# RWKV time mixing: keys and values with features on the partitions, low ranks from the unmixed input, and an earlier token reorder

## The chip, the cores and the metric

One NeuronCore of a Trainium2 chip runs the whole program. The metric is device microseconds (us) of one execution; a kernel's time is the median of its runs. TensorE is called PE below (PEld is its weight load), VectorE is DVE, ScalarE is ACT, GpSimd is POOL, and SP is the SyncE queue that issues every DMA of this kernel.

## What is computed

Two transformer blocks over one sequence of T = 512 tokens with 1024 features. The first block has neighbourhood attention on an 8 x 64 grid of tokens, a gated convolution and an MLP. The second has two layers with a feed-forward net (SwiGLU) ahead of and behind a mixer; the mixer of its first layer is the RWKV-7 time mixing, which the change is about:

```python
x_prev = jnp.pad(x, ((0, 0), (1, 0), (0, 0)))[:, :-1]
xx = x_prev - x
xr, xw, xk, xv, xa, xg = [x + xx * mu[i] for i in range(6)]
r = xr @ w_rkv[0]; k = xk @ w_rkv[1]; v = xv @ w_rkv[2]
w = -jax.nn.softplus(-(w0 + jnp.tanh(xw @ w1) @ w2)) - 0.5
decay = jnp.exp(-jnp.exp(w))
a = jax.nn.sigmoid(a0 + (xa @ a1) @ a2)
g = jax.nn.sigmoid(xg @ g1) @ g2
kk = heads(k * k_k); kk = kk / jnp.maximum(norm(kk), 1e-12)   # per head of 64
k = k * (1.0 + (a - 1.0) * k_a)
# scan over t, per head, S is 64 x 64:
#   S = S * w_t + (S @ -kk_t) b_t^T + v_t k_t^T ;  y_t = S @ r_t
# then group norm, bonus, gate g, and @ w_o
```

w1 and a1 have 64 columns, g1 has 128; the matrices of r, k, v and w_o are 1024 x 1024.

## The kernel before

Activations lie transposed, features on the 128 partitions and tokens along the free dimension, in eight tiles of 128 x 512 (`DC` = 8). The large products are exact to fp32 through a split: `wload` brings 128 x 1024 weights by DMA (`wr`), ACT rounds them to a high part (`wh`), DVE or POOL subtracts for the low part (`wl`), and `mm3` issues three matmuls (high by high, high by low, low by high). The first block runs with its tokens in column order of the grid; the time mixing needs them in sequence.

The program is written as one main stream of products and as side tasks (Python generators). A planner (`_Emit`) places the side tasks between the main products; its result is one fixed order of instructions on each engine, and each engine's queue is then strictly in order. All DMAs go through the SP queue, in order too: a store that waits for its data holds up the loads behind it.

The time mixing (`rwkv`) works in two halves of 256 tokens, hf = 0 and 1. `norm_task` makes, for each feature chunk c, a tile `ud` with u (the normalised input) and its shift difference d. `mix_task` makes the mixtures u + d * mu on DVE: for K, R and V each chunk is also split in high and low (ACT, then POOL or DVE), for the low ranks W, A and G it is not. Then the main stream runs through `ORDER`:

```python
ORDER = [(0, K_), (0, W_), (0, A_), (0, R_), (0, V_), (0, G_), (1, K_), (1, W_), (1, A_), (1, R_), (1, V_), (1, G_)]
```

K and V go through `token_major`: tokens on the partitions, the mixture as the stationary operand, 512 columns of weights moving, four PSUM banks at once; `keys_task` scales, norms and transposes the keys, `values_task` transposes the values. R goes through `receptance`, the other way round: 128 x 128 weights stationary, 256 tokens moving. The low ranks go through `lora1`, fp32 matmuls of 256 tokens by 64 or 128 weight columns whose weights `load_raw` has fetched one or two steps ahead. All results go to DRAM (`spill`) and are fetched again by blocks of 128 tokens j = 0 to 3 and halves of the heads q = 0, 1.

Behind this runs a chain of side tasks for each block j: `prep(q, j)` (DVE and ACT, small matmuls on PE), for which K, the decay, A and R of that half must be there (`flags`), room for 12 tiles must be free, and fewer than two are under way; when both q are done, `inverse(j)`, which inverts 32 x 32 triangles in 31 steps of two dependent POOL instructions, after a trip through DRAM (`fsc` out, `iat` in; `xsc` out and in behind it) and three rounds of 32 x 32 matmuls; `scan_task(q)`, two steps of 64 tokens for each j, each a string of small matmuls and DVE work; and `gn_task`. When j = 0 and 1 are through, `w_o(0)` multiplies the first half by the output matrix, and the following feed-forward net (`ffn_halves`) can start on it; the second half's chain then runs beside that net.

The token reorder stands in the first feed-forward net of the second block, `ffn(0, 0, perm=True)`: DVE's products of the hidden values read and write through strided views (`rows_first`, `natural`), and after the first group of hidden values the eight tiles of the residual `h` are copied into sequence order on ACT, with a second set of row statistics (`Stat`).

Of the kernel before, what the change touches and what calls it, by code (L numbers as in the profile page):

```python
# [12 lines left out]
F32 = mybir.dt.float32  # L13
# [7 lines left out]
P = 128  # L21
# [16 lines left out]
def _vec_layout():  # L38
    col = 0
    for name, n in [  # L40
        ("norm1_g", 8), ("norm2_g", 8), ("norm_g", 96), ("conv_w", 12), ("qk_g", 2), ("mu", 48),
        ("a0", 8), ("k_a", 8), ("r_k", 8), ("gn_g", 8), ("gn_b", 8), ("kv_norm_g", 8),
# [14 lines left out]
R_KK, R_BV, R_SINK = 0, 1024, 1280  # L57
# [238 lines left out]
def tile_net(ctx: ExitStack, tc: tile.TileContext, a: dict, out: bass.AP, dbg=None, stop=None):  # L296
# [438 lines left out]

    for n in range(DC):
# [136 lines left out]
    def rows_first(ap):  # L873

        return ap.rearrange("p (c r) -> p r c", r=8)

    def natural(ap):
        return ap.rearrange("p (r c) -> p r c", c=64)

# [103 lines left out]
    def ffn(layer, i, en, on_h=None, perm=False, on_last=None):  # L983
# [10 lines left out]
        for lo_, hi_ in GROUPS:  # L994
            hid, waits = {}, []

            def hidden(j, pg, pu):
# [7 lines left out]
                def fn():  # L1005
                    s_ = A()
                    if perm:
                        tt(vt, natural(s_), rows_first(pg), rows_first(st.rb), MUL)
                        act.activation(out=s_, in_=s_, func=AF.Silu)
                        tt(vt, natural(s_), rows_first(pu), natural(s_), MUL)  # L1010
                    else:
                        tt(vt, s_, pg, st.rb, MUL)
                        act.activation(out=s_, in_=s_, func=AF.Silu)
                        tt(vt, s_, pu, s_, MUL)
# [24 lines left out]
            if lo_ == 0 and perm:  # L1039
                hp_ = []  # L1040
                st = Stat()
                for c in range(DC):
                    t_ = A()
                    copy(natural(t_), rows_first(h[c]))
                    hp_.append(t_)
                    st.add(t_)
                h = hp_
                st_pre = st
                for hf in range(2):
                    em.spawn(st.task(hf, bcast=False))  # L1050
                st = en.st
# [3 lines left out]
            if lo_ == GROUPS[1][0]:  # L1055
                if perm:
                    em.until(st_pre.all)
                    pre = st_pre.y
                else:
                    pre = st.y  # L1060
                so = Stat(pre=pre, post=0.5)
# [54 lines left out]
    def rwkv(on_h):  # L1116
# [23 lines left out]
        def mix_chunk(i, c, hf):  # L1140

            uc, dc, m = ud[hf, c][:, 0:256], ud[hf, c][:, 256:512], V("mu", 8 * i + c)
            if i in LORA:
                if c % 2 == 0:
                    half_tile[0] = A()
# [1019 lines left out]
```

## Time and profile before

| | us |
|---|---|
| median of 3 runs | 2996.33 |
| runs | 2992.95 to 2996.84 |
| the profiled execution | 2992.11 |
| span of its trace | 2990.3 |
| PE busy in the span | 2832.4 (95%) |
| DVE busy | 1623.5 (54%) |
| ACT busy | 1250.4 (42%) |
| POOL busy | 688.6 (23%) |

The profile is of one execution; 1.8 us of its time lie outside the span. PE is busy nearly throughout, so a stage in which it is not stands out: the time mixing, from about 1043 to 1560 us of the span. A busy PE may still be slow, since the clock that it is granted has two levels; tables by stage therefore list the granted clock (1.00 is 2.4 GHz, 0.50 is 1.2 GHz, in between is a mean).

### The profile page before, as it was taken

Reading aid. Unit: us, or ns where it says so; the run is one execution under the profiler, and the core shown is the slowest. Engines: PE = TensorE matmul, PEld = TensorE weight load, DVE = VectorE, ACT = ScalarE, POOL = GpSimd, SP = SyncE. Lnnn points to the kernel's source line nnn. Section 1 sums busy time; section 2 is a strip of 40 time slices with the busy share of each in tenths; the row PEclk is TensorE's granted clock in tenths of the full one; section 3 lists DMA queues with packets and bytes.
Section 4 is the critical chain, followed back from the end, with each engine's and each line's share of the span. In section 5 each row is a group of like instructions: output and inputs, shape, how many; then the busy total and the mean of one; then the engine's idle time right before and its main releaser. Section 6 shows DMA issues by size and latency. Waiting matters only on the chain. (4 is left out here: it accounts for less than half of the span.)

```text
span 2990.3 us, 45732 instructions
## 1 busy us (share of the span) xinstructions
PE 2832.4 (95%) x17744; PEld 2448.3 (82%) x17744; DVE 1623.5 (54%) x2920; ACT 1250.4 (42%) x2157; POOL 688.6 (23%) x809
## 2 busy tenths in 40 slices
PE   9999999999999988688789999998999998999998
PEld 7788988889788877557669999998888887888887
DVE  6544443335334485775866664457334475852336
ACT  4523333333433345455445544344333347743333
POOL 0011211111211143554254110011111126420111
PEclk9999999999999988889779999999999999999999
DMA  5232333332334355555455655343333333323334
GB/s 186 89 99 92 113 105 93 99 99 85 93 99 125 117 178 171 179 177 163 145 169 156 198 174 178 121 156 86 112 99 123 116 115 86 104 84 102 110 109 154
DMA packets 179408, 378.31 MB, mean 127 GB/s; under 512 B 57204, under 2 KB 81908, under 8 KB 179192
## 3 DMA queue, kind: packets, MB, share of 16 engines
q1 hardware_dynamic: 179192, 375.40, 40.5%
q8 instruction: 140, 2.29, 0.3%
q14 instruction: 76, 0.62, 0.1%
HBM read 342.04 MB, written 29.36 MB: 124 GB/s over the span
## 5 line engine op out<-in xcount | busy, mean ns | idle before, releaser
L377 PE MATMUL m<-a,wh 128*128 128x256 f32 (+1 forms) x8512 | 2068.2, 335 | 7.2 <-DVE a L288 4.8
L377 PEld LDWEIGHTS m<-a,wh 128*128 128x128 f32 x8512 | 1463.7, 192 | 171.8 <-issue 8.4
L377 PE MATMUL m<-a,wl 128*128 128x256 f32 (+1 forms) x4256 | 1415.3, 333 | 3.6 <-DVE wl L288 3.3
L288 ACT ACTIVATE wh<-wr 128x1024 fp32r<-128x1024 f32 (+2 forms) x585 | 606.5, 1038 | 1190.6 <-PE m L377 814.6
L288 DVE TENSOR_TENSOR wl<-wr,wh 128x1024 fp32r<-128x1024 f32 (+2 forms) x547 | 672.6, 1231 | 467.7 <-ACT wh L288 464.6
L377 PEld LDWEIGHTS m<-a,wl 128*128 128x128 f32 x4256 | 816.2, 192 | 79.6 <-DVE wl L288 5.0
L288 POOL TENSOR_TENSOR a<-a,a 128x256 f32<-128x256 f32 (+5 forms) x319 | 361.9, 1141 | 1645.6 <-ACT a L288 1321.6
L288 DVE TENSOR_TENSOR a<-m,a 128x512 f32<-128x512 f32 (+1 forms) x324 | 208.3, 644 | 636.6 <-PE m L377 619.0
L288 ACT ACTIVATE a<-a 128x512 f32<-128x512 f32 (+6 forms) x531 | 253.3, 495 | 120.7 <-DVE a L288 101.1
L377 PE MATMUL m<-wh,a 128*128 128x512 f32 x800 | 269.6, 412 | 22.4 <-POOL a L288 9.5
L377 PEld LDWEIGHTS m<-wh,a 128*128 128x128 f32 x800 | 156.5, 197 | 63.2 <-POOL a L288 11.8
L288 DVE TENSOR_TENSOR a<-a,a 128x256 f32<-128x256 f32 (+3 forms) x305 | 165.5, 569 | 25.1 <-ACT a L288 18.2
L377 PE MATMUL m<-wl,a 128*128 128x512 f32 x400 | 162.6, 406 | 0.2 <-DVE wl L288 0.2
L288 DVE SCALAR_TENSOR_TENSOR a<-a,vec,a 128x256 fp32r<-128x256 f32 (+4 forms) x246 | 147.7, 640 | 8.6 <-ACT a L288 8.3
L288 POOL TENSOR_TENSOR a<-h,a 128x256 fp32r<-128x256 f32 x80 | 68.1, 855 | 293.2 <-ACT a L288 277.8
L288 POOL TENSOR_TENSOR wl<-wr,wh 128x1024 fp32r<-128x1024 f32 x38 | 92.8, 2444 | 129.1 <-ACT wh L288 97.8
L377 PE MATMUL t<-a,a 64*128 64x128 f32 (+4 forms) x528 | 91.8, 361 | 31.8 <-DVE a L288 21.8
L377 PEld LDWEIGHTS t<-a,a 64*128 64x128 f32 (+3 forms) x528 | 59.3, 202 | 57.5 <-issue 24.5
L288 ACT ACTIVATE a<-t 128x512 f32<-128x512 f32 (+3 forms) x122 | 58.5, 490 | 95.3 <-PE t L377 73.3
L377 PEld LDWEIGHTS m<-wl,a 128*128 128x128 f32 x400 | 78.8, 197 | 16.9 <-issue 0.7
L288 ACT ACTIVATE a<-a,vec 128x256 fp32r<-128x256 f32 (+2 forms) x108 | 60.3, 566 | 41.3 <-DVE a L288 39.2
L290 ACT ACTIVATE a<-t 128x256 f32<-128x256 f32 (+3 forms) x100 | 45.5, 473 | 65.4 <-PE t L377 47.3
(108 smaller groups left out, 1527.7 us busy)
## 6 DMA issues: line engine op xcount, KB each, us to landing
wr<-in_ffn_w_in_dram SPq DMA_DIRECT2D x204, 512.0 KB, 3.6
wr<-in_ffn_w_out_dram SPq DMA_DIRECT2D x80, 448.0 KB, 3.3
wr<-in_ffn_w_out_dram SPq DMA_DIRECT2D x48, 512.0 KB, 3.5
wr<-in_w_out_t_dram SPq DMA_DIRECT2D x34, 512.0 KB, 3.3
wr<-in_w_mlp_in_dram SPq DMA_DIRECT2D x32, 512.0 KB, 3.5
wr<-in_w_mlp_out_dram SPq DMA_DIRECT2D x32, 512.0 KB, 3.7
wr<-in_w_gate_dram SPq DMA_DIRECT2D x16, 512.0 KB, 3.6
wr<-in_w_k_dram SPq DMA_DIRECT2D x16, 512.0 KB, 4.4
```

The lines of the kernel that those rows point to most:

```text
L288: return fn(*args, **kw)
L290: return fn(*args, **kw)
L377: nc.tensor.matmul(out_, lhsT=lhsT, rhs=rhs, start=start, stop=stop)
```

## The change

Four edits. (1) K and V go through a new function `features`, the form that R had: eight output chunks n, for each 24 matmuls with 128 x 128 weights stationary and 256 tokens moving, one PSUM bank. `keys` squares the keys on ACT, sums them by head with 128 x 2 matmuls on PE, spreads the inverse norms over features by four transposes for each pair of chunks, and multiplies on DVE out of PSUM; `values` (not shown) copies, stores and transposes back for the token-major copy `vd`. The copies in DRAM (`kt`, `kkt`, `vt`) are now by half and chunk, stored as 128 x 256 tiles and fetched in rows of 128 tokens. (2) The low ranks use u and d themselves: x @ w1 with x = u + d * mu is u @ w1 + d @ (mu * w1). POOL scales the weights by mu (`lora1`), W and A share one product with 64 + 64 columns (`wa1`), and the weights are loaded inside `lora1`. (3) `ORDER` is shorter, `AHEAD` is 12 in place of 8 and `EARLY` 8 in place of 10 (of ten steps, not twelve). (4) The reorder moves to the gated sum of the first block: POOL's addition of the two branches reads `rows_first` and writes `natural`; the residual is read from a copy of x in sequence order (`x_nat`); `perm` is gone.

```diff
-        tt(gp, sg[0], sg[0], sg[1], ADD)
-        mg.append(split(sg[0], eng=gp))
+        t_ = A()
+        tt(gp, natural(t_), rows_first(sg[0]), rows_first(sg[1]), ADD)
+        mg.append(split(t_, eng=gp))
     h = []
     for c in range(DC):
         t_ = A()
-        dma(out=t_, in_=a["x"][:, c * T : (c + 1) * T])
+        dma(out=t_, in_=a["x_nat"][:, c * T : (c + 1) * T])
         h.append(t_)
...
-                    if perm:
-                        tt(vt, natural(s_), rows_first(pg), rows_first(st.rb), MUL)
-                        act.activation(out=s_, in_=s_, func=AF.Silu)
-                        tt(vt, natural(s_), rows_first(pu), natural(s_), MUL)
...
-            if lo_ == 0 and perm:
-                hp_ = []
-                st = Stat()
-                for c in range(DC):
-                    t_ = A()
-                    copy(natural(t_), rows_first(h[c]))
-                    hp_.append(t_)
-                    st.add(t_)
-                h = hp_
-                st_pre = st
-                for hf in range(2):
-                    em.spawn(st.task(hf, bcast=False))
-                st = en.st
...
-        LORA = {W_: ("w1", 64), A_: ("a1", 64), G_: ("g1", 128)}
-        ORDER = [(0, K_), (0, W_), (0, A_), (0, R_), (0, V_), (0, G_), (1, K_), (1, W_), (1, A_), (1, R_), (1, V_), (1, G_)]
-        LAST_A = [x for x in ORDER if x[0] == 0][-1]
-        mixed = {x: [] for x in ORDER}
+        WA_, L_ = W_, (W_, G_)
+        ORDER = [(hf, i) for hf in range(2) for i in (K_, WA_, R_, V_, G_)]
+        MIXED = [x for x in ORDER if x[1] not in L_]
+        mixed = {x: [] for x in MIXED}
...
-        AHEAD = 8
-        EARLY = 10
+        AHEAD = 12
+        EARLY = 8
...
-        def token_major(w, i, hf):
-            pss = {(wh, jj): PS() for wh in range(2) for jj in range(2)}
-            for k0 in range(0, DC, 2):
-                ws = [wload(w[wh][:, k0 * 512 : (k0 + 2) * 512], 1024, eng=alt()) for wh in range(2)]
-                for k in range(k0, k0 + 2):
+        def features(w, i, hf, fin):
+            for n in range(DC):
+                ps = PS()
+                hi, lo = wload(w[n], 1024, eng=alt())
+                for k in range(DC):
                     xh, xl = take(hf, i, k)
-                    sl = slice((k - k0) * 512, (k - k0 + 1) * 512)
-                    for (wh, jj), ps in pss.items():
-                        hi, lo = ws[wh]
-                        tb = slice(jj * 128, (jj + 1) * 128)
-                        em.need(ps, xh[:, tb], xl[:, tb], hi[:, sl], lo[:, sl])
-                        mm3(ps, xh[:, tb], xl[:, tb], hi[:, sl], lo[:, sl], k == 0, k == DC - 1)
-                    used[0] += 1
-                    free(xh)
+                    sl = slice(k * 128, (k + 1) * 128)
+                    em.need(ps, hi[:, sl], lo[:, sl], xh, xl)
+                    mm3(ps[:, HW], hi[:, sl], lo[:, sl], xh, xl, k == 0, k == DC - 1)
+                    if n == DC - 1:
+                        used[0] += 1
+                        free(xh)
+                fin(n, ps)
             mixed[hf, i] = None
-            return pss
...
-        def lora1(w, m, hf, i):
+        def lora1(hf, name, idx):
+            ws = load_raw(a[name], 1024)
+            ms = []
+            for i, w_ in enumerate(ws):
+                m_ = A()
+                w4, m4 = (t_.rearrange("p (k i m) -> p k i m", k=4, i=len(idx)) for t_ in (w_, m_))
+                for x, id_ in enumerate(idx):
+                    c = _VEC["mu"] + 8 * id_ + 4 * i
+                    mu = vec[:, c : c + 4].unsqueeze(2).broadcast_to([P, 4, 128 // len(idx)])
+                    tt(gp, m4[:, :, x, :], w4[:, :, x, :], mu, MUL)
+                ms.append(m_)
             ps = PS()
             for k in range(DC):
-                x_ = take(hf, i, k)[0]
-                w_ = w[k * m // 512][:, k * m % 512 : k * m % 512 + m]
-                em.need(ps[:m, HW], w_, x_)
-                mm(ps[:m, HW], w_, x_, k == 0, k == DC - 1)
-                if k % 2:
-                    used[0] += 1
-                    free(x_)
-            mixed[hf, i] = None
+                em.until(lambda: (hf, k) in ud)
+                for i, t_ in enumerate((ws, ms)):
+                    w_, x_ = t_[k // 4][:, (k % 4) * 128 : (k % 4 + 1) * 128], ud[hf, k][:, HALF[i]]
+                    em.need(ps[:, HW], w_, x_)
+                    mm(ps[:, HW], w_, x_, k == 0 and i == 0, k == DC - 1 and i == 1)
+            free(*ws, *ms)
             return ps
...
+        def keys(hf):
+            st_ = kst[hf] = {"ss": None, "n": 0}
+            def square(n, sq):
+                yield (sq,)
+                if st_["ss"] is None:
+                    st_["ss"] = PS()
+                for jj in range(2):
+                    c = 16 * jj + 2 * n
+                    mm(st_["ss"][:, c : c + 2], sq[:, jj * 128 : (jj + 1) * 128], bones[:, 0:128:64])
+                st_["n"] += 1
+                if st_["n"] == DC:
+                    em.spawn(norm(st_["ss"]))
+            def norm(ps):
+                s1, s2 = S(), S()
+                v, f, tmp = s1[:, 0:32], s2[:, 0:32], s2[:, 32:64]
+                vt.tensor_scalar(out=v, in0=ps[:, 0:32], scalar1=1e-24, scalar2=None, op0=MAX)
+                rsqrt_(f, v, tmp)
+                for n in range(0, DC, 2):
+                    if n % 4 == 0:
+                        fb = [A(), A()]
+                        for jj in range(2):
+                            c = 16 * jj + 2 * n
+                            copy(fb[jj].rearrange("p (h d) -> p h d", d=64), f[:, c : c + 8].unsqueeze(2).broadcast_to([P, 8, 64]))
+                    yield tuple(fb)
+                    pf = PS()
+                    for i in range(2):
+                        for jj in range(2):
+                            x0 = ((n + i) % 4) * 128
+                            transpose(pf[:, i * 256 + jj * 128 : i * 256 + (jj + 1) * 128], fb[jj][:, x0 : x0 + 128])
+                    if n % 4 == 2:
+                        free(*fb)
+                    k_ = kt.pop((hf, n // 2))
+                    for i in range(2):
+                        kk = H()
+                        vt.scalar_tensor_tensor(out=kk, in0=k_[:, HALF[i]], scalar=V("k_k", n + i), in1=pf[:, HALF[i]], op0=MUL, op1=MUL)
+                        spill(kkd[hf][n + i], kk)
+                    free(k_)
+                    if n % 4 == 2:
+                        flags["k", hf, n // 4] = True
+            def fin(n, ps):
+                if n % 2 == 0:
+                    kt[hf, n // 2] = A()
+                t_, sq = kt[hf, n // 2][:, HALF[n % 2]], H()
+                copy(t_, ps[:, HW])
+                act.activation(out=sq, in_=ps[:, HW], func=AF.Square, scale=V("k_k", n))
+                spill(kd_[hf][n], t_)
+                em.spawn(square(n, sq))
+            return fin
...
-        tasks = {W_: decay_task, A_: a_task, G_: g_task}
-        raw = {}
         for n, (hf, i) in enumerate(ORDER):
-            for nxt in ORDER[n : n + 2]:
-                if nxt[1] in LORA and nxt not in raw:
-                    w, m = LORA[nxt[1]]
-                    raw[nxt] = load_raw(a[w], 8 * m)
             if not hv and n >= EARLY and min(done["z"]) >= 1:
                 w_o(0)
-            if i in LORA:
-                em.spawn(tasks[i](hf, lora1(raw[hf, i], LORA[i][1], hf, i)))
-                free(*raw[hf, i])
+            if i == WA_:
+                ps = lora1(hf, "wa1", (W_, A_))
+                em.spawn(decay_task(hf, ps))
+                em.spawn(a_task(hf, ps))
+            elif i == G_:
+                em.spawn(g_task(hf, lora1(hf, "g1", (G_,))))
+                free(*(ud[hf, c] for c in range(DC)))
             elif i == K_:
-                em.spawn(keys_task(hf, token_major(a["w_k"], K_, hf)))
+                features(a["w_k"], K_, hf, keys(hf))
             elif i == V_:
-                em.spawn(values_task(hf, token_major(a["w_v"], V_, hf)))
+                features(a["w_v"], V_, hf, values(hf))
             else:
-                receptance(hf)
+                features(a["w_r"], R_, hf, receptance(hf))
...
-        ffn(0, 0, en, en_r.add, perm=True, on_last=lambda: next(mixing))
+        ffn(0, 0, en, en_r.add, on_last=lambda: next(mixing))
```

What the edits do to the order of the queues shows at three places. On SP, the place is the end of the first half's keys. Before, the weights of the first low rank (`in_w`) were issued ahead of the last key weights and of all key stores:

```order
L288 DMA wr_8932<-in_w_k_dram 128x1024
L288 DMA wr_8976<-in_w_k_dram 128x1024
L288 DMA a_8741<-in_w_dram 128x512
L288 DMA xsc_8727<-a_8731 128x512 x2
L288 DMA xsc_8728<-a_8731 128x512 x2
L288 DMA xsc_8729<-a_8731 128x512 x2
L288 DMA xsc_8730<-a_8731 128x512 x2
L288 DMA wr_8982<-in_w_k_dram 128x1024
```

Now, on SP at the same place of the program (`kt` is the store of the keys, `in_wa` the joint weights of W and A):

```order
L288 DMA kt_5533<-a_8964 128x256
L288 DMA wr_9437<-in_w_r_dram 128x1024
L288 DMA kt_5533<-a_9074 128x256
L288 DMA wr_9471<-in_w_r_dram 128x1024
L288 DMA kt_5533<-a_9074 128x256
L288 DMA a_9136<-in_wa_dram 128x512
L288 DMA a_9137<-in_wa_dram 128x512
L288 DMA wr_9509<-in_w_r_dram 128x1024
```

The joint weights have moved behind the store of the last key chunk.

On POOL, the place is the end of the first `inverse` (tiles `iat` and its X). Before, the second one followed at once:

```order
L288 TENSOR_TENSOR h_10635<-a_9968,iat_9967 128x16
L288 TENSOR_TENSOR a_9968<-a_9968,h_10635 128x16
L288 MEMSET a_10588 128x512
L288 MEMSET a_10588 64x16 x2
L288 TENSOR_TENSOR h_10721<-a_10588,iat_10587 128x31
L288 TENSOR_TENSOR a_10588<-a_10588,h_10721 128x31
```

Now other work follows the first inverse on POOL (`a<-a,vec` scales low-rank weights, `h<-h,s` is the scan's, `wl` are weights of R and V, 22 rows in all up to the second inverse):

```order
L288 TENSOR_TENSOR h_10680<-a_10079,iat_10078 128x16
L288 TENSOR_TENSOR a_10079<-a_10079,h_10680 128x16
L288 TENSOR_TENSOR wl_11530<-wr_11528,wh_11529 128x1024
L288 TENSOR_TENSOR a_10798<-h_10796,a_10798 128x256
L288 TENSOR_TENSOR a_10814<-h_10812,a_10814 128x256
L288 TENSOR_TENSOR a_10854<-h_10852,a_10854 128x256
L288 TENSOR_TENSOR a_10859<-h_10857,a_10859 128x256
L288 TENSOR_TENSOR wl_11746<-wr_11744,wh_11745 128x1024
L288 TENSOR_TENSOR a_10876<-a_10872,vec 128x4x64 x2
L288 TENSOR_TENSOR a_10879<-a_10873,vec 128x4x64 x2
```

The second inverse has moved behind the scan's first two steps and the weights of the first V chunks of the second half.

On PE, the place is the first 32 x 32 round of the second inverse. Before, it stood amid the R products of the second half (`m<-a,wh` and `m<-a,wl`):

```order
L377 MATMUL m_11686<-a_10826,wh_11688 128x256 x2
L377 MATMUL m_11686<-a_10826,wl_11689 128x256
L377 MATMUL m_11686<-a_10922,wh_11688 128x256
L377 MATMUL t_11394<-cst,a_11390 32x32 x16
L377 MATMUL m_11686<-a_10922,wh_11688 128x256
L377 MATMUL m_11686<-a_10922,wl_11689 128x256
L377 MATMUL m_11686<-a_10995,wh_11688 128x256
```

Now, on PE, it stands behind the last V product (`m_12382`) and the bonus and transposes of the values:

```order
L377 MATMUL m_12382<-a_11953,wh_12384 128x256 x2
L377 MATMUL m_12382<-a_11953,wl_12385 128x256
L377 MATMUL t_12404<-a_12309,cst 128x512
L391 MATMUL t_12428<-cst,a_12254 128x128 x2
L391 MATMUL t_12436<-cst,a_12254 128x128 x2
L391 MATMUL t_12428<-cst,a_12379 128x128
L391 MATMUL t_12436<-cst,a_12379 128x128
L391 MATMUL t_12428<-cst,a_12379 128x128
L391 MATMUL t_12436<-cst,a_12379 128x128
L377 MATMUL t_12333<-cst,a_12329 32x32 x16
L377 MATMUL t_12463<-h_12460,a_10463 32x32 x16
```

Between that row and the first row of `w_o(0)` PE's queue now holds small matmuls of side tasks and the 16 of the low rank G, no R or V product any more.

## Rows read from the trace of the kernel before

**Rows 1.** The page's first part: busy us, share of the span, instructions.

```profile
span 2990.3 us, 45732 instructions
PE 2832.4 (95%) x17744; PEld 2448.3 (82%) x17744; DVE 1623.5 (54%) x2920; ACT 1250.4 (42%) x2157; POOL 688.6 (23%) x809
```

**Rows 2.** Busy time by stage: window, PE, PEld, DVE, ACT, POOL, granted clock, DMA.

```profile
1409.00:1500.00 91.00, 66.15 (x447) 52.58 (x448) 78.39 (x167) 42.75 (x96) 25.78 (x33) 0.76 0.48 146
1043.00:1560.00 517.00, 420.04 (x3188) 338.94 (x3186) 369.38 (x726) 248.00 (x513) 221.30 (x327) 0.86 0.55 169
```

**Rows 3.** PE's waits from 1040 to 1560 us: us, times, longest.

```profile
PE t L377 <- DVE a L288: 31.3, 18, 7.0
PE m L377 <- DVE a L288: 9.5, 4, 4.0
```

**Rows 4.** Timeline of PE: start, us, instruction, count, idle before it.

```profile
809.43 1.05 PE L377 MATMUL t<-cst,a 128*128 128x1 f32 x8 [2.73 <-POOL a L288]
...
1136.75 8.48 PE L377 MATMUL m<-a,a 128*64 128x256 f32 x32 [4.04 <-DVE a L288]
1145.16 0.50 PE L377 MATMUL m<-a,wh 128*128 128x256 f32 x2
...
1382.11 0.69 PE L377 MATMUL t<-cst,a 32*32 32x32 f32 x32
...
1499.50 0.59 PE L377 MATMUL m<-a,wh 128*128 128x256 f32 x2
```

**Rows 5.** Busy time of stretches with 512 and with 256 moving columns.

```profile
975.00:1000.00 25.00, 25.00 (x112) 20.72 (x111) 10.18 (x10) 8.57 (x13) 4.88 (x5) 1.00 0.29 91
1875.00:1900.00 25.00, 25.00 (x211) 25.00 (x210) 12.31 (x16) 8.98 (x11) 0.74 (x1) 1.00 0.52 159
```

**Rows 6.** DVE by line and shape, 1040 to 1560 us: busy us, mean ns.

```profile
L288 DVE SCALAR_TENSOR_TENSOR a<-a,vec 128x256 f32<-128x256 f32 x48 | 23.9, 529 | 0.1
...
L288 DVE TENSOR_TENSOR a<-a,s 128x512 f32<-128x512 f32 x8 | 6.1, 758 | 0.2
L288 DVE TENSOR_TENSOR a<-a,row 128x512 f32<-128x512 f32 x8 | 6.0, 748 | 19.5 <-PE t L391 19.5
...
L288 DVE TENSOR_TENSOR a<-m,row 128x512 f32<-128x512 f32 x8 | 5.1, 679 | 4.3 <-ACT a L288 4.3
...
L288 DVE TENSOR_REDUCE s<-a 128x8 f32<-128x512 f32 x8 | 5.1, 672 | 0.0
```

**Rows 7.** POOL by shape, and a DMA issue (KB, us to landing), 1040 to 1560 us.

```profile
L288 POOL TENSOR_TENSOR a<-a,a 128x256 f32<-128x256 f32 x20 | 18.4, 924 | 35.0 <-ACT a L288 34.4
...
a<-in_g_dram SPq DMA_DIRECT2D x8, 256.0 KB, 4.8
```

**Rows 8.** Timeline of DVE and SP: first prep, and load of the first inverse.

```profile
1187.24 0.95 DVE L288 SCALAR_TENSOR_TENSOR a<-a,a 128x512 f32<-128x512 f32 x1 [3.33 <-DMA a<-ad]
...
1237.71 1.10 SPq L288 DMA_DIRECT2D iat<-fsc  x2
```

**Rows 9.** Timeline of POOL: first and last step of inverse 0, then of inverse 1.

```profile
1247.10 0.24 POOL L288 TENSOR_TENSOR h<-a,iat 128x31 f32<-128x31 f32 x1
...
1305.96 0.23 POOL L288 TENSOR_TENSOR a<-a,h 128x16 f32<-128x16 f32 x1
...
1311.40 0.24 POOL L288 TENSOR_TENSOR h<-a,iat 128x31 f32<-128x31 f32 x1 [4.40 <-DMA iat<-fsc]
...
1367.45 0.23 POOL L288 TENSOR_TENSOR a<-a,h 128x16 f32<-128x16 f32 x1
```

**Rows 10.** The tile of the inverses: POOL's instructions, duration ns min/median/max.

```profile
L288 POOL TENSOR_TENSOR h<-a,iat x124: 218/398/1324, 1247.1 to 1608.0; 128x126 f32<-128x126 f32 x12, 128x30 f32<-128x30 f32 x8, 128x56 f32<-128x56 f32 x8, 128x78 f32<-128x78 f32 x8
```

**Rows 11.** Timeline at the last gated sum: POOL's addition, DVE's subtractions.

```profile
279.88 1.29 POOL L288 TENSOR_TENSOR a<-a,a 128x512 f32<-128x512 f32 x1 [12.80 <-DVE a L288]
...
274.52 1.22 DVE L288 TENSOR_TENSOR wl<-wr,wh 128x1024 fp32r<-128x1024 f32 x1 [0.15 <-ACT wh L288]
...
279.96 2.29 DVE L288 TENSOR_TENSOR wl<-wr,wh 128x1024 fp32r<-128x1024 f32 x1 [0.16 <-ACT wh L288]
```

More of the change, by code (lines that the diff above doesn't have):

```diff
@@ L1055, in ffn @@
             if lo_ == GROUPS[1][0]:
[L1056 to L1061, printed above, removed]
+                so = Stat(pre=st.y, post=0.5)
             if lo_ == 0:
@@ L1179, in mix_task @@
         def mix_task():
-            for hf, i in ORDER:
+            for hf, i in MIXED:
                 for c in range(DC):
-                    while made[0] >= used[0] + (AHEAD if (hf, i) in ORDER[:4] else 8) or (hf, c) not in ud or not room(MARGIN[0]):
+                    while made[0] >= used[0] + AHEAD or (hf, c) not in ud or not room(MARGIN[0]):
                         yield 0.25
                     mixed[hf, i].append(mix_chunk(i, c, hf))
-                    made[0] += i not in LORA or c % 2
-                    if hf == 1 and i == ORDER[-1][1]:
-                        free(ud[1, c])
-                    if hf == 0 and (hf, i) == LAST_A:
-                        free(ud[0, c])
+                    made[0] += 1
                     yield mixed[hf, i][max(c - 2, 0)]
@@ L1259, in keys_task, with values, turn @@
+        def values(hf):
+            vs = []
+            def turn(q, ts):
+                for jj in range(2):
+                    yield tuple(ts)
                     ps = PS()
-                    yield (ps, kraw[n])
                     for c in range(4):
-                        transpose(ps[:, c * 128 : (c + 1) * 128], kraw[n][:, c * 128 : (c + 1) * 128])
-                    t_ = A()
-                    copy(t_, ps)
-                    spill(dst[wh, 2 * hf + jj], t_)
-                    free(t_)
@@ L1267, in keys_task, with fin @@
-                free(kraw[n])
-                flags["k", hf, wh] = jj == 1
+                        transpose(ps[:, c * 128 : (c + 1) * 128], ts[c // 2][:, (c % 2) * 256 + jj * 128 : (c % 2) * 256 + (jj + 1) * 128])
+                    v_ = A()
+                    copy(v_, ps)
+                    spill(vd[hf][jj * 128 : (jj + 1) * 128, q * 512 : (q + 1) * 512], v_)
+                    free(v_)
+                free(*ts)
+                flags["v", hf, q] = True
+            def fin(n, ps):
+                if n % 2 == 0:
+                    vs.append(A())
+                t_ = vs[-1][:, HALF[n % 2]]
+                copy(t_, ps[:, HW])
+                spill(vtd[hf][n], t_)
+                if n % 4 == 3:
+                    em.spawn(turn(n // 4, vs[-2:]))
@@ L1295, in decay_task, with load_raw @@
             flags["lg", hf] = True
[L1297 removed]
+        def load_raw(src, n, rows=slice(0, P)):
             ts = [A() for _ in range(0, n, 512)]
             for i, t_ in enumerate(ts):
[L1301 removed]
+                dma(out=t_[rows, :], in_=src[:, 512 * i : 512 * i + 512])
             return ts
```

132 lines of the change are left out of this document (38 added, 94 removed).

## The prediction

> **What bounds the kernel now.** I read the page's first part: PE is busy 95% of the span [rows 1], so almost everywhere PE's own work is the time, and a change that adds PE work there costs it in full. The table by stage shows the exception. In the time mixing, from 1043 to 1560 us, PE is busy 420.0 of 517 us and its mean granted clock is 0.86 [rows 2]: 97 us of waiting, and 0.14 x 517 = 72 us that went by the slower clock, which shows here after waits (some of the 72 falls into them). DVE is busy 369.4 us there, 78.4 of 91 at its end from 1409 to 1500. The waits of PE say who ended them: DVE's `a` tiles for 31.3 and 9.5 us [rows 3]. So the stage is bound by a chain through DVE and POOL that blocks PE's fixed order, not by PE's work.
>
> The timelines give that chain its places, for the first half of the tokens: the keys end at 1136.75 - 4.04 = 1132.7, R begins at 1145.2 [rows 4], the first `prep` starts on DVE at 1187.2, the load of the first inverse is issued at 1237.7 [rows 8]. POOL steps through inverse 0 from 1247.1 to 1306.2 and inverse 1 from 1311.4 to 1367.7 [rows 9]; PE's 32 x 32 round for inverse 1 comes at 1382.1, `w_o(0)` begins at 1499.5 [rows 4]. Behind `w_o(0)` a feed-forward net fills PE, so the moment at which `w_o(0)` starts is what the change can move.
>
> **The change, part by part.** *Reorder.* Before, PE waits 2.73 us once for the copied residual's statistics, at 809.43 [rows 4]; that goes: -2.7. The strided products on DVE lie beside a saturated PE and count nothing. The gated sum's addition takes 1.29 us on POOL at the last chunk [rows 11]. POOL's strided form is not shown in the trace; I take no loss, since PE's next product has 21 matmuls of 223 ns = 4.7 us before it needs that chunk; without that cover an addition of twice the length costs 1.3.
>
> *K and V as features.* 384 matmuls of 512 columns become 768 of 256. A stretch of the first kind holds 112 in 25.00 us, 223 ns each; of the second 211, 118.5 ns [rows 5]: 85.6 against 91.0 us, +5.4 us of PE work. In the second kind PEld is busy all 25.00 us, in the first 20.72. The Trainium skill (TensorE: Matmul & The Clock Gate, LDWEIGHTS and Back-to-back issue gap) says that loading weights takes their columns over 1.2 GHz, about 107 ns, however many columns then move, and gives 262 and 518 cycles for the two widths: it speaks against halving the width, since weight load and product are then equally long. By its cycles the edit adds an estimated 0.9 us, by the rows 5.4; the trace agrees with the direction, and I keep the rows.
>
> *Low ranks.* 48 fp32 products of 256 tokens become 64. 16 of them, each shown as two matmuls, took 8.48 us at 1136.75 [rows 4], 0.53 each: +8.5, and twice that at half the clock. The 32 transposes that fall away and the 32 two-column products that come I set equal; at 0.12 us each (a short matmul, rows 5) they are within 4 us. So PE gets some 14 us more work, under 97 us of waits. If that cover were gone, 14 would be the loss.
>
> *DVE.* Gone are 48 mixtures (23.9 us), 8 each of the products by `row` out of PSUM (5.1) and SBUF (6.0), by the norms (6.1), and the sums (5.1) [rows 6]: 46.2. New are 16 products of 128 x 256 out of PSUM, at the mixtures' 529 ns 8.5. Net -37.7 of 369.4. *POOL* gets 8 scalings of 128 x 256 at 0.92 us [rows 7] and 4 of 128 x 512 at 1.29 [rows 11], +12.6 of 221.3. *ACT* exchanges full-width copies for twice as many of half the width; busy 248 of 517 [rows 2], it counts nothing. SP has 17 DMAs more, small stores; they matter through the order.
>
> *The order*, walked along the chain (estimates from the rows named). **Keys end:** all eight chunks are now needed before the first output is done, but the last mixture stands at the same place of DVE's queue and the other seven outputs run on prepared weights: 1132.7 less 2.7, 1130. **R begins:** the joint weights are loaded behind the last key store. Store and issue about 0.5, landing 4.8, two scalings 1.8 [rows 7], then 16 products at 0.53 and transposes for the norm: 1130 + 7 + 8.5 + 2 = 1148, 3 later than before. This is the wait that takes the place of the mixtures' 4.04. **First prep:** before, 42 us after R began, with the keys' transposes between R's products and PE cold. R itself is 192 x 0.1185 = 22.8; the prep's loads stand behind R's sixth store, 17 us, and I add as much again for the decay and A matmuls: 1182 (bound: 42 again, 1190). **Load of inverse 0:** 50.5 us after, less the eight G mixtures that stood there (4.2): 1228. **Inverse 0:** 9.4 for the trip as before, 59 us of steps with other POOL work between; I count about as many such rows now, with fewer waits for ACT, and take 52: 1238 to 1290. **Inverse 1:** here the order turns against the change. Before, it followed at once; now the fourth `prep` stands on DVE behind the norms of the second half's keys and the first scan steps. From 1290, 14.7 for the trip to PE (as 1367.5 to 1382.1), 5 for queued stores, 4.8 landing, 50 rows of DVE at its mean of 369.4/726 = 0.51, 25.5, then the trip of 9.4: 1350, 39 later than before. POOL is then free of other work: 62 steps of 0.40 [rows 10] and 5 for gaps, 30: 1380, and the 32 x 32 round at 1395, 13 later than before. **w_o(0):** before 117 us after that round, with V's matmuls and 86% of DVE between. Now V is done; 113 rows of DVE stand from the next scan step to `w_o(0)`, at 78.4/167 = 0.47 each 53, and I add 10 for the three rounds and 12 for waits: 75, so 1470. Bounds: 117 less V's 96 x 0.223 = 21.4 gives 1491; 65 without waits gives 1460.
>
> Sum: 1470 against 1499.5, -29.5 (the 2.7 is in it), bounds -8.5 and -39.5. Behind it nothing is moved that PE waits for. The profiled execution took 2992.1 (span 2990.3 [rows 1] and 1.8 around it); 2962.6 from it. The median of the runs is 4.2 above that execution, so 2967 is the forecast, its own range 2950 to 2990.
>
> **The rivals.** *Inverse 1 comes too late (slower).* `w_o(0)` follows its start by 30 + 14.7 + 75 = 120 us in my walk, so the change loses from the point where inverse 1 starts after 1499.5 - 120 = 1380. For it: the fourth prep needs 12 free tiles while 4 more mixtures are held, its loads stand behind stores that wait, and no R or V product is left to fill PE, so the clock falls too. Against: 30 us of room. At 1402 it gives +22: 3018.
> *No change.* The last stretch stays DVE's, 117 us from the round; with the round 13 later and V's 21 gone, and cold PE after the idle time, -8 to +6: 2990 to 3002. Against: DVE has 37.7 less to do.
> *DVE was all of it.* All 40.8 us of waits for it go, and with denser work some 20 of the 72 lost by the clock: 2935. Against: preps, scans and norms, the most of DVE's work, stay.
> *POOL's scaling holds DVE up.* Beside POOL's addition at 279.88 DVE's subtraction took 2.29 us, at 274.52 alone 1.22 [rows 11]: 1.07 lost while both ran. If each new POOL operation costs DVE its length, 12.6 of the gain goes: 2980. The Trainium skill (SBUF — State Buffer, Who interferes with whom) states it as an exclusive lock between a DVE instruction with two SBUF inputs and a POOL instruction that reads SBUF; by that rule, the trace agrees.
>
> **How the numbers follow.** The walk 0.47, POOL's hold 0.10, DVE in full 0.12, no change 0.15, inverse 1 too late 0.16. Within 0.2%, about what a measurement of this kernel can tell from no change, is 2990 to 3002. The first three are faster (0.69), and of "no change" 0.05 more; 0.07 of it is the same and 0.03 slower, with 0.02 of the walk the same: faster 0.72, same 0.09, slower 0.19. The range leaves out the late inverse and the far end of the third: 2938 to 3004.
>
> **What would show it.** In the changed profile: R's first matmul about 1148, behind an idle time ended by POOL; the first load of `iat` near 1228; inverse 1's first step near 1350 (after 1380 the first rival holds); PE idle and cold ahead of the 32 x 32 round near 1395; `w_o(0)` near 1470; DVE some 38 us less busy in the stage, PE some 14 more at full clock. The prediction is wrong if `w_o(0)` no longer starts the dense work, or if waits for the low-rank weights show at all four places with more than 7 us.

## The result and the profile after

The changed kernel takes 3028.11 us (median of 4 runs, 3027.04 to 3031.75), the kernel before, run beside it, 2994.64: ratio 1.0114, 95% interval 1.0097 to 1.0132. It is slower by 33 us; 2967 was forecast. The profiled execution took 3031.75 with a span of 3030.0, 39.7 longer than that of before.

The page's first part of the changed kernel answers to [rows 1]:

```profile
span 3030.0 us, 46575 instructions
PE 2857.5 (94%) x18184; PEld 2502.4 (83%) x18184; DVE 1587.2 (52%) x2832; ACT 1241.3 (41%) x2161; POOL 692.9 (23%) x814
```

DVE lost 36.3 us of work, as the change meant, and PE got 25.1 us more busy time (some 14 at full clock were forecast; its mean granted clock over the span fell from 0.967 to 0.957). Neither explains 39.7 by itself; the table by stage does (columns as in [rows 2]):

```profile
1043.00:1560.00 517.00, 408.46 (x3218) 357.67 (x3217) 311.08 (x595) 232.36 (x485) 218.91 (x318) 0.81 0.52 159
1290.00:1386.00 96.00, 85.88 (x850) 71.14 (x849) 46.29 (x104) 46.42 (x94) 26.15 (x30) 0.78 0.51 152
1500.00:1560.00 60.00, 28.97 (x209) 22.41 (x207) 32.31 (x85) 14.29 (x37) 30.98 (x71) 0.56 0.31 83
```

In the time mixing PE is now idle 108.5 us of 517 (before 97) and its mean granted clock is 0.81 (before 0.86). DVE is busy 311, 60% of the stage in place of 71%, so it is no longer what is short. The last stretch is the worst one: from 1500 to 1560 no engine is busy more than 33 of 60 us, and what PE does there runs at a clock of 0.56, near the lower of its two levels. That is a chain with nothing left to put beside it.

PE's waits from 1040 to 1560 us (us, times, longest), which answer to [rows 3], say whose chain:

```profile
PE t L391 <- POOL a L290: 28.4, 2, 19.2
PE m L377 <- POOL a L288: 13.2, 5, 5.3
PE t L377 <- DVE a L288: 12.9, 7, 4.7
```

The larger of the two DVE rows of [rows 3] fell from 31.3 to 12.9 us; new is POOL's part of the group norm (L290), which follows the scan, with 28.4. Before, that wait was:

```profile
PE t L391 <- POOL a L290: 1.2, 1, 1.2
```

PE's timeline has the places of [rows 4]:

```profile
1145.44 1.22 PE L377 MATMUL m<-a,a 128*128 128x256 f32 x2 [5.86 <-DMA a<-in_wa_dram]
...
1157.83 0.59 PE L377 MATMUL m<-a,wh 128*128 128x256 f32 x2
...
1456.91 0.69 PE L377 MATMUL t<-cst,a 32*32 32x32 f32 x32 [0.16 <-DMA a<-xsc]
...
1549.30 1.12 PE L391 MATMUL t<-cst,a 128*128 128x128 f32 x4 [19.23 <-POOL a L290]
...
1559.60 1.12 PE L391 MATMUL t<-cst,a 128*128 128x128 f32 x4 [9.18 <-POOL a L290]
...
1560.37 1.42 PE L377 MATMUL m<-a,wh 128*128 128x256 f32 x5
```

R begins at 1157.8 (1145.2 before), the 32 x 32 round of inverse 1 comes at 1456.9 (1382.1), and the last row is the start of `w_o(0)`: 1560.4, 61 us later than before. Of the 61, 21 come back behind it (the span grew by 39.7); where was not taken apart. POOL's timeline, for [rows 9], shows where the 75 us of the round come from:

```profile
1247.09 0.24 POOL L288 TENSOR_TENSOR h<-a,iat 128x31 f32<-128x31 f32 x1 [1.27 <-DMA iat<-fsc]
...
1292.95 0.23 POOL L288 TENSOR_TENSOR a<-a,h 128x16 f32<-128x16 f32 x1
...
1400.97 0.24 POOL L288 TENSOR_TENSOR h<-a,iat 128x31 f32<-128x31 f32 x1
...
1438.55 0.23 POOL L288 TENSOR_TENSOR a<-a,h 128x16 f32<-128x16 f32 x1
```

Inverse 0 starts when it did and ends 13 us earlier. Inverse 1 starts 108 us after that; before, it followed at once. It waits for the fourth `prep`. The first step of that prep on DVE, before and after:

```profile
1269.46 0.69 DVE L288 SCALAR_TENSOR_TENSOR a<-a,a 128x512 f32<-128x512 f32 x1
```

```profile
1336.06 0.69 DVE L288 SCALAR_TENSOR_TENSOR a<-a,a 128x512 f32<-128x512 f32 x1 [0.38 <-DMA a<-ad]
```

Its loads are issued only at 1330.7 on SP, behind the stores of the second half's normed keys and the loads of its second-stage low ranks:

```profile
1320.02 4.42 SPq L288 DMA_DIRECT2D kkt<-h  x8
...
1329.48 1.15 SPq L288 DMA_DIRECT2D a<-in_a_dram  x2
1330.69 0.60 SPq L288 DMA_DIRECT2D a<-kkt  x1
```

So the second half's keys and joint low rank went ahead of the first half's last prep. Theory A: the planner did that because the prep must find 12 of the pool's 56 tiles free, and something now holds them. Rivals: B, the feature form costs; C, the waits for the low ranks' weights cost.

### The profile page after: what moved, and what is told of

Read it like the earlier page. It is cut to its first block, busy times and chain, and to the rows that moved or that the text cites. A ratio compares the mean times of both kernels' runs of the same rounds, so it can differ in the third digit from the quotient of the medians.

```text
span 3030.0 us, 46575 instructions
## 1 busy us (share of the span) xinstructions
PE 2857.5 (94%) x18184; PEld 2502.4 (83%) x18184; DVE 1587.2 (52%) x2832; ACT 1241.3 (41%) x2161; POOL 692.9 (23%) x814
## 5 line engine op out<-in xcount | busy, mean ns | idle before, releaser
L377 PE MATMUL m<-a,wh 128*128 128x256 f32 (+1 forms) x9024 | 2176.6, 333 | 27.4 <-POOL a L288 10.1
L377 PEld LDWEIGHTS m<-a,wh 128*128 128x128 f32 x9024 | 1556.1, 193 | 192.2 <-POOL a L288 14.4
L377 PE MATMUL m<-a,wl 128*128 128x256 f32 (+1 forms) x4512 | 1493.9, 332 | 1.1 <-DVE wl L288 1.0
L377 PEld LDWEIGHTS m<-a,wl 128*128 128x128 f32 x4512 | 871.9, 193 | 78.0 <-DVE wl L288 1.7
L288 ACT ACTIVATE a<-a 128x256 f32<-128x256 f32 (+6 forms) x507 | 234.7, 479 | 109.7 <-DVE a L288 84.6
L377 PE MATMUL m<-wh,a 128*128 128x512 f32 x544 | 170.9, 392 | 2.5 <-DVE a L288 1.5
L377 PE MATMUL t<-a,a 64*128 64x128 f32 (+3 forms) x528 | 94.7, 364 | 13.5 <-DVE a L288 11.3
L377 PE MATMUL m<-wl,a 128*128 128x512 f32 x272 | 106.1, 390 | 0.0
L377 PEld LDWEIGHTS t<-a,a 64*128 64x128 f32 (+2 forms) x528 | 61.3, 202 | 32.0 <-issue 13.5
L288 ACT ACTIVATE a<-m 128x256 f32<-128x256 f32 (+2 forms) x134 | 63.3, 475 | 41.6 <-PE m L377 40.9
L391 PE MATMUL t<-cst,a 128*128 128x128 f32 x224 | 40.2, 320 | 41.5 <-POOL a L290 28.4
```

What stands on the lines that cost most here:

```text
L288: return fn(*args, **kw)
L377: nc.tensor.matmul(out_, lhsT=lhsT, rhs=rhs, start=start, stop=stop)
L391: nc.tensor.transpose(out_, in_, ident[: in_.shape[0], : in_.shape[0]])
```

## The experiments

Ratios are to the kernel before, run beside each experiment (its medians lie between 2995.4 and 2996.8 us), with the 95% interval; "first step" is the first step of inverse 1 on POOL.

**reorder_only.** The kernel before with edit 4:

```diff
-        tt(gp, sg[0], sg[0], sg[1], ADD)
+        tt(gp, natural(t_), rows_first(sg[0]), rows_first(sg[1]), ADD)
-        ffn(0, 0, en, en_r.add, perm=True, on_last=lambda: next(mixing))
+        ffn(0, 0, en, en_r.add, on_last=lambda: next(mixing))
```

> The kernel before with edit 4 alone (the reorder in the gated sum). Theory A, late inverse: the loss of 33 us is none of this edit's; the 2.73 us wait goes, 2992. Rival, the strided addition on POOL: at the last chunk PE waits longer than it gains, 2996 or more.

2989.89 us, 0.9978 (0.9966 to 0.9990); first step 1306.9. The edit is a gain of its own, 6.7 us.

**features_only** and **lowranks_only** are the changed kernel with edits taken back: edits 2 and 3 (low ranks, order and depths) in the first, edit 1 (the features) in the second. One place of each:

```diff
-                ps = lora1(hf, "wa1", (W_, A_))
+                em.spawn(tasks[i](hf, lora1(raw[hf, i], LORA[i][1], hf, i)))
```

```diff
-                features(a["w_k"], K_, hf, keys(hf))
+                em.spawn(keys_task(hf, token_major(a["w_k"], K_, hf)))
```

> The kernel before with edits 1 and 4: keys and values by features, low ranks still from mixtures, twelve steps, AHEAD 8. Theory A (the low ranks hold the tiles of u and d to the end of a half, so that the fourth prep waits for twelve free tiles): here inverse 1 starts before 1350 us, and the time is 2970 to 2995. Theory B (the feature form costs: half the columns for each weight load, and a key norm that needs all eight chunks): 3010 or more here.

> The kernel before with edits 2, 3 and 4: low ranks from u and d, ten steps, AHEAD 12, keys and values still with 512 columns moving. Theory A: inverse 1 starts after 1380 us and the time is 3010 to 3040. Theory B: inverse 1 stays near 1311 and the time is 2980 to 2997. Theory C (the low ranks cost through the wait for their weights alone, some 13 us at four places): 3003 to 3010, with inverse 1 within 15 us of before.

features_only: 2996.20, 1.0001 (0.9992 to 1.0010), first step 1304.7, 1 us above theory A's range. lowranks_only: 3031.25, 1.0122 (1.0106 to 1.0138), first step 1410.3. The whole loss is in edits 2 and 3, and it comes with the late inverse.

**hold_mixtures.** The changed kernel, in which the second half's mixtures leave room for the preps until four of them have begun (`nprep` counts them):

```diff
-  while made[0] >= used[0] + AHEAD or (hf, c) not in ud or not room(MARGIN[0]):
+  while made[0] >= used[0] + AHEAD or (hf, c) not in ud or not room(14 if hf and nprep[0] < 4 else MARGIN[0]):
```

> The changed kernel, but until the fourth prep has started the mixtures of the second half are only made where 14 tiles are free (2 before). Theory A: the fourth prep comes ahead of the second half's keys, inverse 1 starts before 1350 us, and the time is 2990 or less. Theories B and C: the loss stays, 3020 or more; keys that wait for their mixtures could add some us.

2993.26, 0.9997 (0.9987 to 1.0006). Its POOL row:

```profile
1322.66 0.24 POOL L288 TENSOR_TENSOR h<-a,iat 128x31 f32<-128x31 f32 x1 [8.30 <-DMA iat<-fsc]
```

Inverse 1 starts 78 us earlier and 35 us of the time come back, with every operation of the change in place. Theory A holds for the loss. The time fell 3 us short of the 2990 expected.

**ahead12_only** and **lowranks_ahead8** ask what holds the tiles: AHEAD 12, or the tiles of u and d that the new low ranks keep. The first is reorder_only, the second lowranks_only, with one number changed:

```diff
-        AHEAD = 8
+        AHEAD = 12
-  while made[0] >= used[0] + (AHEAD if (hf, i) in ORDER[:4] else 8) or (hf, c) not in ud or not room(MARGIN[0]):
+  while made[0] >= used[0] + AHEAD or (hf, c) not in ud or not room(MARGIN[0]):
```

```diff
-        AHEAD = 12
+        AHEAD = 8
```

> The kernel before with edit 4 and with AHEAD 12 in place of 8 throughout; keys, values and low ranks as before. Theory A1 (the twelve mixtures made ahead take the tiles that the fourth prep needs): inverse 1 starts after 1380 us and the time is 3010 to 3030. Theory A2 (the tiles of u and d, which the new low ranks keep to the end of each half, take them): inverse 1 starts within 20 us of 1307, and the time is 2985 to 2995.

> lowranks_only with AHEAD 8 in place of 12. Theory A1: inverse 1 starts before 1355 us and the time is 2985 to 3000, near reorder_only's 2990 plus what the low ranks cost on PE. Theory A2: inverse 1 stays after 1380, and the time 3015 or more.

ahead12_only: 3026.20, 1.0090 (1.0074 to 1.0107):

```profile
1390.45 0.39 POOL L288 TENSOR_TENSOR h<-a,iat 128x31 f32<-128x31 f32 x1 [0.63 <-DMA iat<-fsc]
```

One number in the old kernel, no other edit of the time mixing, makes the loss: +36 against reorder_only. lowranks_ahead8: 3009.10, 1.0035 (1.0023 to 1.0046), first step 1320.1: the inverse is in time again and 22 us come back, but not all of it; the low ranks at AHEAD 8 cost 19 against reorder_only in another way.

**early_weights** and **early_weights_hold.** The load and the scaling leave `lora1` and are issued ahead of the fourth of the eight outputs of K and of V, without and with the held mixtures:

```diff
             for n in range(DC):
+                if n == 3 and i in NEXT:
+                    weights(hf, *NEXT[i])
```

> The changed kernel, but the low ranks' weights are loaded and scaled five chunks before the end of the keys (and of the values). Theory C (the waits for these weights are on the path): the waits for in_wa and in_g, 11 us, and part of those for POOL go, and the time falls to 3008 to 3018. Theory A (only the late inverse counts): inverse 1 still starts after 1380 us, and the time stays within 3020 to 3032.

> hold_mixtures with the low ranks' weights loaded and scaled five chunks earlier. If the waits for these weights (13 us in hold_mixtures) are on its path, 2980 to 2986; if other work would have been waited for anyway, 2990 to 2998.

early_weights: 3007.02, 1.0027 (1.0013 to 1.0040), 21 us below the changed kernel, which theory A alone (3020 to 3032) does not allow, and 1 us below theory C's range (3008 to 3018). R begins 12.7 us earlier, and inverse 1 is as late as ever:

```profile
1145.15 0.59 PE L377 MATMUL m<-a,wh 128*128 128x256 f32 x2
...
1530.51 0.78 PE L377 MATMUL m<-a,wh 128*128 128x256 f32 x2
```

```profile
1395.80 0.24 POOL L288 TENSOR_TENSOR h<-a,iat 128x31 f32<-128x31 f32 x1
```

The second row is `w_o(0)`: 30 us earlier than in the changed kernel, although inverse 1 starts only 5 earlier. So with a late inverse the weights cost 21 us, more than theory C's 11 to 13. Where they do is argued, not shown: both loads were moved at once. POOL stood idle for the second half's G in the changed kernel,

```profile
1461.04 2.04 POOL L288 TENSOR_TENSOR a<-a,vec 128x512 f32<-128x512 f32 x2 [22.26 <-DMA a<-in_g_dram]
```

but PE had other work at that time (no wait above 0.5 us from 1456 to 1484). Two things differ on PE: G's products stand behind the 32 x 32 round in the changed kernel (1463.3 to 1474.6) and ahead of it here (1413.9 to 1425.4), and the wait for POOL's group norm, 28.4 us there, is shorter:

```profile
PE t L391 <- POOL a L290: 15.1, 1, 15.1
```

early_weights_hold: 2991.83, 0.9977 (0.9966 to 0.9988), first step 1311.4; only 1.4 us below hold_mixtures, against the 2980 to 2986 expected if the waits for the weights were on the path. Its `w_o(0)` begins 25 us earlier all the same, at 1471.6 for 1496.4, and ahead of the second half's G; the load of the residual (`hsp`), which stands behind the first product of `w_o(0)`, confirms the place:

```profile
1471.60 0.80 PE L377 MATMUL m<-a,wh 128*128 128x256 f32 x2
```

```profile
1475.30 0.39 SPq L288 DMA_DIRECT2D a<-hsp  x1
```

So the early weights do bring `w_o(0)` forward, and the gain is lost behind it (below).

**What the feature form costs.** features_only lost 6 us against reorder_only. Theory D puts that on the keys, whose seven other outputs follow the last mixture. Five kernels take the keys or the values, or both, back to 512 columns, with the early weights and held mixtures kept, two of them with AHEAD 8; a sixth takes the held mixtures away; values_alone puts the values' new form into reorder_only. With the diff of lowranks_only for K, V or both (in the old form the early weights stand ahead of the third of eight chunks):

> The low ranks from u and d, without the features edit (keys and values with 512 columns moving), AHEAD 8, with early weights and with mixtures held as in early_weights_hold. Theory D (the feature form costs: the keys end some 7 us later since seven outputs follow the last mixture, and PE has 5 us more): 2980 to 2987, below early_weights_hold. Theory E (the feature form is free or pays, by what it takes from DVE): 2990 or more. Against reorder_only this run says what the low ranks are worth when nothing waits for tiles or weights.

> early_weights_hold with the keys back in their old form (512 columns moving, four banks), values still by features. Theory D in the part on the keys' end: R begins some 8 us earlier than in early_weights_hold, and the time falls to 2983 to 2988. If the width of the values' products were what costs, 2990 to 2994.

> reorder_only with the values by features; keys and low ranks as before. Theory D (of the features edit the keys' part costs, since seven of eight outputs follow the last mixture, and the values' part pays, since it moves work off DVE and out of the stretch behind inverse 1): 2978 to 2988, below reorder_only's 2990 and 8 or more below features_only's 2996. If the 256-column form itself costs: 2992 to 2998 here too, about half of features_only's loss at the least.

> values_only_early_hold with AHEAD 8 in place of 12, so that it differs from lowranks_early_hold by the values' form alone. If the ten us between those two came from the values' form, 2964 to 2971 here; if they came from AHEAD, 2975 to 2981.

> lowranks_early_hold with AHEAD 12: neither keys nor values by features, the corner that was missing beside values_only_early_hold (2968) and early_weights_hold (both by features, 2992). If the values' form is what made 2968: 2976 to 2984. If it was AHEAD 12 with held mixtures: 2962 to 2972, and the values' form is worth nothing.

> early_weights_hold with the values back in their old form, keys by features. If the keys' form costs wherever it stands (the second half's keys ended 26 us later with it): 2985 to 3000, near early_weights_hold. If the cost was one order's accident: 2965 to 2980.

> values_only_early_hold without holding mixtures: the fourth prep again waits for tiles. Theory A: inverse 1 starts after 1375 us and the time rises by 15 to 35, to 2983 to 3003. If its 2968 came from the keys' and values' forms alone: 2965 to 2972.

| kernel | by features | us | ratio (interval) | first step |
|---|---|---|---|---|
| neither_early_hold | - | 2982.13 | 0.9954 (0.9938 to 0.9969) | 1317.4 |
| values_only_early_hold | V | 2968.09 | 0.9902 (0.9887 to 0.9917) | 1312.7 |
| keys_only_early_hold | K | 2991.64 | 0.9981 (0.9971 to 0.9991) | 1316.1 |
| early_weights_hold | K, V | 2991.83 | 0.9977 (0.9966 to 0.9988) | 1311.4 |
| values_only_early (not held) | V | 3018.71 | 1.0070 (1.0051 to 1.0088) | 1413.4 |
| lowranks_early_hold (AHEAD 8) | - | 2977.70 | 0.9932 (0.9917 to 0.9948) | 1328.5 |
| values_early_hold_ahead8 | V | 2987.64 | 0.9975 (0.9963 to 0.9988) | 1314.0 |
| values_alone (reorder_only + V) | V | 3006.51 | 1.0027 (1.0016 to 1.0037) | 1312.0 |

At AHEAD 12 the keys' form costs 9.5 us with old values and 23.7 with new ones, and the values' form gains 14 with old keys and nothing with new ones. At AHEAD 8 it costs 10, and on the old low ranks 16.6 (values_alone, where 2978 to 2988 was expected). On the old low ranks the keys' form gains 10 (features_only 2996.2 against values_alone 3006.5). So theory D fell: neither form has a price of its own, although keys_only_early_hold, taken alone, came where a fixed price of the keys would put it. The R beginning that was expected 8 us earlier in values_only_early_hold came at 1149, some 3 later than in early_weights_hold. Outside what was expected lie also lowranks_early_hold (2980 or more), values_only_early_hold (2983 to 2994), values_early_hold_ahead8 (2964 to 2981) and values_only_early (2983 to 3003).

Two findings stand. Taking the held mixtures away from the fastest kernel puts inverse 1 back 101 us and costs 50.6:

```profile
1413.42 0.24 POOL L288 TENSOR_TENSOR h<-a,iat 128x31 f32<-128x31 f32 x1
```

And values_only_early_hold is 27 us faster than the kernel before. In its time mixing PE is busy 433 us at 0.87, and `w_o(0)` begins at 1470.4:

```profile
1043.00:1560.00 517.00, 433.18 (x3370) 372.01 (x3368) 366.17 (x703) 256.84 (x533) 248.94 (x350) 0.87 0.58 176
```

```profile
1470.36 0.59 PE L377 MATMUL m<-a,wh 128*128 128x256 f32 x2
```

## Why the prediction was wrong

The likeliest case was wrong; the rival "inverse 1 comes too late" (0.16) is what happened. By its own terms: it was to decide from a first step after 1380, at 1402 to cost 22 and to end at 3018; the first step came at 1401.0 and the time is 3028. That the two lie so close is partly luck: `w_o(0)` followed the first step by 159 us, not by 120, and 21 us of its delay came back behind it.

**The step that failed: inverse 1.** The prediction put it at 1350, from inverse 0's end at 1290 by 14.7 of trip, 5 of stores, 4.8 of landing, 50 rows of DVE at 0.51 (25.5) and 9.4 of trip. Inverse 0 did end at 1293.2. The 60 us became 108: 43 to the first prep step at 1336 (24.5 allowed), 49.7 from there to the inverse's load at 1385.7 (25.5), 15.2 from the load to the first step (9.4). The loads of inverse 0 and inverse 1:

```profile
1242.41 1.09 SPq L288 DMA_DIRECT2D iat<-fsc  x2
...
1385.73 1.11 SPq L288 DMA_DIRECT2D iat<-fsc  x2
```

The error was to price the rows in between by DVE's mean. From 1290 to 1386 DVE was busy 46.3 of 96 us, PE 85.9 at a clock of 0.78: the prep's small matmuls and the key norm stood in PE's queue between the products of the second half. Of the 50 us in which DVE stood idle PE ended 31, most of it in these rows:

```profile
DVE h L288 <- PE t L377: 9.6, 2, 7.2
DVE h L288 <- PE t L391: 7.9, 2, 7.7
```

So PE, more than DVE, set the pace of the stretch. That the order had changed was read correctly; which engine would price the new order was not.

**w_o(0).** The step took 75 us from the 32 x 32 round, because V would be done. It took 103.5 (1456.9 to 1560.4). PE's last matmul of the scan ended at 1530.1, 73 us after the round; for what followed the sum had no term. PE waited 28.4 us for POOL's rows of the group norm, which stood in POOL's queue between the steps of the next block's inverse 2; before, they were through when inverse 2 began. The changed kernel, then before:

```profile
1526.17 0.42 POOL L288 TENSOR_TENSOR h<-a,iat 128x31 f32<-128x31 f32 x1
...
1535.74 1.04 POOL L290 TENSOR_TENSOR a<-a,s 128x512 f32<-128x512 f32 x1
...
1558.24 1.31 POOL L290 TENSOR_TENSOR a<-a,s 128x512 f32<-128x512 f32 x1
```

```profile
1482.26 1.36 POOL L290 TENSOR_TENSOR a<-a,s 128x512 f32<-128x512 f32 x1 [8.61 <-ACT a L288]
...
1493.47 0.24 POOL L288 TENSOR_TENSOR h<-a,iat 128x31 f32<-128x31 f32 x1 [4.45 <-DMA iat<-fsc]
```

DVE had delivered for the first of these rows at 1528.3 and for the last at 1552.4; POOL came to them 7.4 and 5.9 us later. What this costs in all no run separates. In early_weights the step took 71 (1459.7 to 1530.5).

The credit for V was an error of another kind: V stood ahead of the round only because the round was late. Where inverse 1 came in time, V stood behind the round again: in early_weights_hold inverse 1 ended at 1365.4 and `w_o(0)` began at 1471.6, 106 later, where the walk has 14.7 and 75.

**What w_o(0) moves.** The prediction took the start of `w_o(0)` for the time, since behind it nothing was moved that PE waits for. That premise did not hold either. In the changed kernel 21 of 61 us came back. early_weights_hold and values_only_early_hold begin `w_o(0)` at 1471.6 and 1470.4, as the walk forecast (1470), but their times are 2992 and 2968. The difference lies behind: from 1560 to 1800 us, in the kernel before, early_weights_hold and values_only_early_hold:

```profile
1560.00:1800.00 240.00, 232.24 (x2389) 222.53 (x2390) 164.31 (x302) 129.09 (x233) 72.18 (x95) 0.96 0.58 175
```

```profile
1560.00:1800.00 240.00, 220.64 (x2346) 209.28 (x2345) 149.47 (x282) 117.88 (x222) 66.99 (x107) 0.91 0.53 155
```

```profile
1560.00:1800.00 240.00, 233.16 (x2584) 225.03 (x2583) 157.10 (x276) 129.89 (x236) 62.95 (x86) 0.99 0.60 174
```

In early_weights_hold PE is busy 221 us at 0.91, in the other 233 at 0.99. Whether the G behind `w_o(0)` makes this was not tested.

**Keys end, R begins.** 1130 was forecast, the last key product ended at 1136.7. All eight outputs need the last mixture, and the other seven, some 20 us of PE, follow it; in the old form only the last chunk's products did. R began at 1157.8 in place of 1148: the 6.7 us of that, 8.8 us from the last key product to the low rank's first one (7 allowed; 5.86 of it waits for the weights), and 12.4 of products and transposes (10.5 allowed; 1.55 of it waits for the scaling).

**Inverse 0.** 1238 to 1290 forecast, 1247.1 to 1293.2 measured: the prep started as late as R did, and the steps were faster than assumed.

**DVE.** -37.7 forecast; over the span -36.3. Right in sum, and partly by luck: 7.3 of it is the reorder's (DVE is busy 1616.2 us in reorder_only), which was not counted, and some 12 were lost beside POOL (next paragraph). Worth little here: its waits on PE's path fell, and others took their place.

**POOL.** 12.6 us of scalings were forecast, 8.9 measured (8 at 635 ns, 4 at 1042). The rival "POOL's scaling holds DVE up" was right that POOL holds DVE up, but not by the scalings. In the time mixing DVE's subtraction of 128 x 1024 grew from 1239 to 1489 ns and that of 128 x 256 from 498 to 823 ns, 34 x 0.25 + 12 x 0.325 = 12.4 us. The ten that took 0.4 us or more above the usual each ran beside a subtraction of POOL's, of which there are as many as before; one of the ten touched a scaling. DVE by line and shape from 1040 to 1560 us, before and after:

```profile
L288 DVE TENSOR_TENSOR wl<-wr,wh 128x1024 fp32r<-128x1024 f32 x40 | 49.5, 1239 | 45.7 <-ACT wh L288 45.6
...
L288 DVE TENSOR_TENSOR a<-h,a 128x256 fp32r<-128x256 f32 x12 | 6.0, 498 | 4.0 <-ACT a L288 4.0
```

```profile
L288 DVE TENSOR_TENSOR wl<-wr,wh 128x1024 fp32r<-128x1024 f32 x34 | 50.5, 1489 | 70.4 <-ACT wh L288 57.4 <-DMA a<-rd 9.1 <-PE m L377 3.5
...
L288 DVE TENSOR_TENSOR a<-h,a 128x256 fp32r<-128x256 f32 x12 | 9.9, 823 | 3.2 <-ACT a L288 3.1
```

An example from the changed kernel, POOL first, then DVE, whose subtraction takes 0.41 us with POOL idle:

```profile
1309.19 2.37 POOL L288 TENSOR_TENSOR wl<-wr,wh 128x1024 fp32r<-128x1024 f32 x1 [5.02 <-ACT wh L288]
```

```profile
1123.54 0.41 DVE L288 TENSOR_TENSOR a<-h,a 128x256 fp32r<-128x256 f32 x1
...
1309.76 2.08 DVE L288 TENSOR_TENSOR a<-h,a 128x256 fp32r<-128x256 f32 x1 [1.35 <-ACT a L288]
```

DVE's ends at 1311.84, just after POOL's at 1311.56. The Trainium skill (SBUF — State Buffer, Who interferes with whom) has this as an exclusive lock on a shared port pair; by that rule, the trace agrees. That it cost no time is likely, since DVE stood idle 206 of the 517 us, but no run shows it.

**Reorder.** -2.7 forecast, -6.7 measured (reorder_only): the first key product comes 4.0 us earlier in its trace (1086.1 for 1090.1), and the first inverse 5.8 (1241.3 for 1247.1); how the 2.7 of the wait becomes 4.0 at the keys was not taken apart.

**Still open.** Why low ranks at AHEAD 8 without early weights (3009) and values_alone (3006) are slow with inverse 1 in time, what makes the values' form worth -14 to +17 by the kernel around it, and what takes back the early `w_o(0)` of early_weights_hold. All differ by an order of some hundred side tasks, so one run for each does not name a place.

## What to carry to other kernels

A depth of prefetch and a task that waits for room draw on one pool: raising the first can starve the second, and the loss then appears far off, in whatever waits for that task. Here 8 to 12 cost 36 us, and giving the critical task first claim on the tiles took 35 and 51 us back. When an order moves work past the critical chain, price each stretch by the engine that is busy in it, give no credit for work that stands ahead only because the chain is late, and look at what stands ahead of the chain's last operations in each engine's queue. The start of a later stage stands for the time only while nothing behind it moves.

## What was not expected of the hardware

With nothing beside it the scan's tail ran at a low clock as well: from 1500 to 1560 us PE's granted clock was 0.56, with idle times of up to 19 us between its matmuls, against 0.76 in the tail of before [rows 2], where V's products ran between the steps.
